# ScalarE's sigmoids of a head pair in a fixed order, and a shorter head start for the next keys, in a stick-breaking attention stage

## The chip, the cores and the metric

The kernel is one program on one core of a Trainium2 chip. Its engines are TensorE (PE in the profile; PEld is its weight load), VectorE (DVE), ScalarE (ACT), GpSimd (POOL) and SyncE (SP, whose queue issues the DMAs). The metric is the time of one execution on the device in microseconds, and smaller is better. A change is judged by the medians of the kernels before and after.

## The reference

A trunk of two layers over 512 tokens of 1024 channels: layer 0 mixes tokens by multi-scale pooling, layer 1 by stick-breaking attention with 16 heads of 64, and each is followed by a squared-ReLU MLP of 4096. All is fp32. The change lies in the attention, which is computed for blocks of 128 queries:

```python
z = jnp.einsum('bhqd,bhkd->bhqk', q_blk, k_blk, preferred_element_type=jnp.float32) * inv_sqrt_d
mask = s_idx < t_idx
log1m = jnp.where(mask, -jax.nn.softplus(z), 0.0)
excl = lax.cumsum(log1m, axis=3, reverse=True) - log1m
a = jnp.where(mask, jnp.exp(jax.nn.log_sigmoid(z) + excl), 0.0)
outs.append(jnp.einsum('bhqk,bhkd->bhqd', a, v_blk.astype(jnp.float32)))
```

So each weight is sigmoid(z) times the product of 1 - sigmoid(z) = sigmoid(-z) over the later keys.

## The kernel before

Every fp32 product is made of three matmuls on a high and a low part: high by high, high by low, low by high. Each evacuation of such an operand is therefore two instructions: ScalarE copies the high part out of PSUM, and VectorE subtracts it from the source to get the low part.

**The attention stage** runs over eight pairs of heads. TensorE works strictly in the order of `ATT_ORDER`, where each word is one step and its number the pair:

- `K` (`start`, L942) begins the projection of the keys of a pair: three of the eight blocks of 128 channels, with three matmuls each. It takes a PSUM bank that stays in use until the projection is finished.
- `P` (`queries_keys`, L962, through `project`, L947) finishes the keys and makes the queries. The copies to `kh`, `kl`, `qh`, `ql` are L967 and L968.
- `S` (`weights`, L1087) makes the scores. `scores` (L1084) fills three banks for each head: query block 3, query block 2, and blocks 1 and 0 together. The two heads alternate on TensorE. Each head then has `against` (L1007), the negated sigmoids into `u`, four instructions; `for_` (L1019), the plain sigmoids into `w`, three instructions; `scan` (L1023) on VectorE, which needs all of the head's `u`; and `weigh` (L1029) on VectorE, which multiplies `w` by the scan's result `e`. There is one buffer `e`, so the second head's scan comes after the first head's weighing.
- `T` (`transposed`) turns the weights of both heads, ten transposes for each head (L1042) into three banks, and evacuates them to `ah` and `al` (L1048 and L1052).
- `A` (`mix_pair`) multiplies by the values (L1059), one bank for each head, and copies the result out (L1066, L1070).
- `V`, `O` and `H` make values (L311 to L313, L898 and L899), output projections (L456 is their first evacuation) and the first values.

The order begins `P0 K1 S0 P1 T0 K2 S1 A0 P2 T1 K3 S2 A1 P3 O001 T2`; from pair 3 on there is no `K`, and the values' projections stand between the steps.

On the engines other than TensorE the order within this stage is chosen when the program is built, by a planner that simulates the run and takes what is ready, by the kernel's own sequence where several are. `tc.manual_schedule(engines=...)` fixes the order of the named engines to that of the code. A helper that splits weights while they are loaded has the lines L170 (ScalarE) and L172 (VectorE); a helper `split` has L292 and L293.

**PSUM** has one pool for all matmul results, with eight buffers of one bank each:

```python
psum = pool("psum", 8, space=bass.MemoryType.PSUM)
def ps():
    return psum.tile([P, 512], F32, tag="ps", name=name("ps"))
```

A buffer is handed to the next that asks once all its readers are done. The readers of a score bank are the head's `against` and `for_` of that bank.

Of the kernel before, what the change touches and what calls it, by code (L numbers as in the profile page):

```python
# [17 lines left out]
S = 512  # L18
T = S // P
KC = D // P  # L20
# [37 lines left out]

ATT_ORDER = [
    (w[0], int(w[1]), [int(c) for c in w[2:]])  # L60
    for w in """H001 N2 H101 N3 H023 H123 P0 K1 S0 P1 T0 K2 S1 A0 P2 T1 K3 S2 A1 P3 O001 T2 O023 S3 A2 P4 V20 T3 V21
    S4 A3 P5 V22 T4 V23 S5 A4 P6 V30 T5 V31 S6 A5 V323 P7 T6 E1""".split()
]

# [41 lines left out]
def trunk(ctx, tc, x, consts, grow, pw, wup, wdn, wq, wk, wv, wo, out):  # L106
# [12 lines left out]
    def name(s):  # L119
        uid[0] += 1  # L120
        return f"{s}{uid[0]}"

    def ps():
        return psum.tile([P, 512], F32, tag="ps", name=name("ps"))
# [22 lines left out]
    def gain_row(r, t=None):  # L147
        t = work.tile([P, D], F32, tag="grow", name=name("grow")) if t is None else t
        nc.sync.dma_start(t, grow[r : r + 1, :].broadcast_to((P, D)))
        return t  # L150
# [87 lines left out]
    def make():  # L238
        k, src, scaled = queue.pop(0)
        if k in kept:  # L240
            made[k] = place(k)
            for n, t in enumerate(made[k]):
                latest["sp"] = nc.sync.dma_start(t.bitcast(F32), kept[k][n])
            return
        made[k] = weight(src, place(k), scaled, dn_raw.pop(k, None))

    def fill(n=1):
        if gate[0]:
            behind.update(latest)
        for _ in range(n):  # L250
            if queue and len(made) < ahead and (queue[0][0][0] != "dn" or dn_pool[0]):
                make()

    def get(key):
        while key not in made:
            make()
        return made.pop(key)

    for l in range(2):
        if l == 1:  # L260
            n = len(queue)
# [180 lines left out]
    def need(*tiles):  # L442
        for t in tiles:
            if t in pending:
                pending.pop(t).transpose()
# [268 lines left out]
    def up_block(pu, w, cols, last=False, ks=range(KC)):  # L714
        wh = w[0].rearrange("p (k c) -> p k c", k=KC)
        wl = w[1].rearrange("p (k c) -> p k c", k=KC)

        def low(k):
            nc.tensor.matmul(pu[:, cols], wl[:, k, :], xnh[:, k, cols], start=False, stop=k == KC - 1)  # L719

        for k in ks:
            nc.tensor.matmul(pu[:, cols], wh[:, k, :], xnh[:, k, cols], start=k == 0, stop=False)  # L722
            nc.tensor.matmul(pu[:, cols], wh[:, k, :], xnl[:, k, cols], start=False, stop=False)  # L723
            if not last:
                low(k)
        if last:
            for k in range(KC):
                low(k)
# [161 lines left out]
    with tc.tile_pool(name="att", bufs=1, reuse_waits="tile") as ap:  # L890
# [14 lines left out]
        def half_values(i, part):  # L905


            if not half_w:
                half_w.extend(get(("v", 0, h)) for h in range(4))
                for u in range(2):  # L910
                    vs[u] = None, value_tile(u)
            for s in part:
                if i == 0:
                    half_bank[s] = ps()
                for k in range(4 * i, 4 * i + 4):
                    (wh, wl), c = half_w[k // 2], NS[k % 2]
                    mm3(
                        half_bank[s], xnh[:, k, TS[s]], xnl[:, k, TS[s]], wh[:, c], wl[:, c], k == 0, k == KC - 1
                    )
                if i == 1:  # L920
                    for u in range(2):
                        value_parts(vs[u][1], s, half_bank[s][:, u * 256 : u * 256 + 256])
            if i == 1 and T - 1 in part:
                fill(ahead)

        def values(u, part):
            if u not in vs:
                vs[u] = [get(("v", u, h)) for h in range(2)], value_tile(u)
            w, v = vs[u]
            for s in part:  # L930
                pv = ps()
                for k in range(KC):
                    c = slice((k % 4) * 256, (k % 4) * 256 + 256)
                    mm3(
                        pv[:, :256], xnh[:, k, TS[s]], xnl[:, k, TS[s]],
                        w[k // 4][0][:, c], w[k // 4][1][:, c], k == 0, k == KC - 1,
                    )
                value_parts(v, s, pv[:, :256])

        started = {}  # L940

        def start(key):  # L942

            started[key] = ps(), get(key)
            up_block(*started[key], slice(0, S), ks=range(3))

        def project(key):  # L947
            if key in started:
                pq, w = started.pop(key)
                up_block(pq, w, slice(0, S), ks=range(3, KC))  # L950
            else:
                pq = ps()
                up_block(pq, get(key), slice(0, S))
            return pq
# [7 lines left out]
        def queries_keys(p):  # L962
            both = []
            for what in "kq":
                src = project((what, p))
                hi, lo = qk_tile(f"{what}h"), qk_tile(f"{what}l")
                latest["act"] = nc.scalar.copy(hi, src)  # L967
                latest["dve"] = nc.vector.tensor_tensor(out=lo, in0=src, in1=hi.bitcast(F32), op=ALU.subtract)  # L968
                both.append((hi, lo))
                fill()  # L970
            return both
# [100 lines left out]
        def scores(hs, b):  # L1072


            (kh, kl), (qh, ql) = hs[0].qk
            for x in hs:
                x.pz[b] = ps()
            o = 0
            for i in Head.SCORES[b][0]:
                n = SEG[i][1]  # L1080
                for m, (x, y) in enumerate(((qh, kh), (qh, kl), (ql, kh))):
                    for h in hs:
                        own = half[h.a]
                        nc.tensor.matmul(  # L1084
                            h.pz[b][:, o : o + n], x[own, TS[i]], y[own, :n], start=m == 0, stop=m == 2,
                        )
                o += n  # L1087

        def weights(p):
            hs = [Head(qk[p], p, a) for a in range(2)]  # L1090
            for b in range(3):
                scores(hs, b)
            for x in hs:
                for b in range(3):
                    x.against(b)
            hs[0].scan()
            for x in hs:
                for b in range(3):
                    x.for_(b)
            hs[0].weigh()  # L1100
            hs[1].scan()
            hs[1].weigh()
            return hs

        def transposed(hs):
            for x in hs:
                for b in range(3):
                    x.turn(b)
                    x.high(b)
                    x.low(b)  # L1110
# [11 lines left out]
        def mix_pair(p, v):  # L1122
            o = o_tile()
            for x in heads[p]:
                x.products(v)
                x.out_low(o)
                x.out(o)
            os[p] = pair_tile(p)
            split(o, *os[p])
# [3 lines left out]
        def out_proj(u, tiles):  # L1133
            if u not in wos:
                wos[u] = [get(("o", 2 * u + c)) for c in range(2)]
            contract([os[2 * u + c] for c in range(2)], wos[u], y, u == 0, tiles)
# [115 lines left out]
        def until(key):  # L1252
            while key not in made:
                make()

        qk, heads, gpost1 = {}, {}, None

        def step(what, i, part):
            nonlocal gpost1
            if what == "H":  # L1260
                half_values(i, part)
            elif what == "V":
                values(i, part)
            elif what == "N":
                need(i)
            elif what == "K":
                start(("k", i))
            elif what == "P":
                qk[i] = queries_keys(i)
                if i == PAIRS - 1:  # L1270
                    until(("o", 5))
            elif what == "S":
                gate[0] = True
                heads[i] = weights(i)
                fill()
            elif what == "T":
                transposed(heads[i])
                behind.update(latest)
            elif what == "A":
                mix_pair(i, vs[i // 2][1])  # L1280
            elif what == "O" and part:
                out_proj(i, part)
                if gpost1 is None:
                    with tc.issue_after(latest["sp"].ins):
                        gpost1 = gain_row(R_MIX_POST1)
# [66 lines left out]
```

## Time and profile before

| | us |
|---|---|
| median of 3 runs | 953.41 (951.75 to 953.63) |
| the profiled execution, its own time | 952.13 |
| its span, first to last instruction | 950.4 |
| PE busy | 936.5 |
| DVE busy | 695.2 |
| ACT busy | 559.2 |

The span is what the trace covers; 1.7 us of the profiled execution lie around it. PE busy counts modelled ends of pipelined matmuls, so the distance between the starts of two instructions tells more than the busy time. A row of the timeline has the start, the time to the end of the last instruction of the row, the engine, the line, what is written and read, the shape and the number of instructions; in brackets stands idle time of the engine just before it and what ended that. One row can hold several instructions of a kind. Numbers of pairs are not in the rows: they follow from the order.

### The profile page before, as it was taken

How to read it: one execution, taken by the hardware profiler on the slowest of the kernel's cores; microseconds unless marked ns; L12 is line 12 of the kernel's file. 1: busy time of each engine (PE TensorE's matmuls, PEld its weight loads, DVE VectorE, ACT ScalarE, POOL GpSimd, SP SyncE). 2: the span in 40 equal slices, each digit the busy share in tenths (PEclk: the TensorE clock that was granted, in tenths of full speed). 3: DMA queues.
4: the chain of work that ended last, by engine and by line, in shares of the span. 5: the costliest groups of instructions: out<-in, count | busy, mean ns of one | idle time of the engine just before them, and what ended most of it. 6: DMA issues, size and time to landing. Idle time of an engine off the chain costs nothing.

```text
span 950.4 us, 12326 instructions
## 1 busy us (share of the span) xinstructions
PE 936.5 (99%) x4702; PEld 789.3 (83%) x4702; DVE 695.2 (73%) x797; ACT 559.2 (59%) x983; POOL 41.3 (4%) x83
## 2 busy tenths in 40 slices
PE   9999999999999999999999999999999999999996
PEld 6998888888888888877888988898888888888885
DVE  5865799988978976258466678884696966958756
ACT  6667979788775646156544444875545444444532
POOL 2300000000000004000000000200000000000002
PEclk9999999999999999999999999999999999999999
DMA  8254969789697850630434271342513233133102
GB/s 308 94 180 144 345 220 345 294 286 352 214 326 264 302 184 2 222 133 1 148 141 161 106 266 45 133 156 71 195 43 130 94 133 111 45 133 111 37 9 90
DMA packets 43262, 156.15 MB, mean 164 GB/s; under 512 B 4289, under 2 KB 4673, under 8 KB 43202
## 3 DMA queue, kind: packets, MB, share of 16 engines
q1 hardware_dynamic: 43202, 155.36, 45.9%
q8 instruction: 37, 0.61, 0.2%
q14 instruction: 23, 0.19, 0.1%
HBM read 121.79 MB, written 33.55 MB: 163 GB/s over the span
## 4 chain that ended last, share of the span: by engine, by line
PE 94%; DVE 2%; ACT 1%; DMA 1%; POOL 1%; issue 0%; SPq 0%; POOLq 0%; DVEq 0%; ACTq 0%
PE ps L600 28%; PE ps L722 15%; PE ps L719 15%; PE ps L723 15%; PE ps L311 4%; PE ps L313 4%; PE ps L312 4%; PE ps L1059 2%; PE ps L1042 2%; PE ps L1084 2%; PE ps L840 1%; PE ps L406 1%; DMA band<-in_consts 1%; PE ps L812 1%; DVE e L1023 1%; ACT xn L296 1%
## 5 line engine op out<-in xcount | busy, mean ns | idle before, releaser
L600 PE MATMUL ps<-w,a 128*128 128x512 f32 x1176 | 278.6, 389 | 0.0
L722 PE MATMUL ps<-xnh,w 128*128 128x512 f32 (+1 forms) x704 | 260.1, 371 | 0.0
L723 PE MATMUL ps<-xnl,w 128*128 128x512 f32 (+1 forms) x704 | 259.8, 370 | 0.0
L719 PE MATMUL ps<-xnh,w 128*128 128x512 f32 (+1 forms) x704 | 259.1, 370 | 0.1
L600 PEld LDWEIGHTS ps<-w,a 128*128 128x128 f32 x1176 | 220.7, 188 | 45.9
L719 PEld LDWEIGHTS ps<-xnh,w 128*128 128x128 f32 x704 | 132.2, 188 | 23.0 <-DVE w L861 0.3
L723 PEld LDWEIGHTS ps<-xnl,w 128*128 128x128 f32 x704 | 132.7, 189 | 22.1
L722 PEld LDWEIGHTS ps<-xnh,w 128*128 128x128 f32 x704 | 132.3, 188 | 22.3
L609 DVE TENSOR_TENSOR y<-ps,y 128x512 f32<-128x512 f32 x124 | 84.2, 686 | 44.1 <-PE ps L600 44.0
L172 DVE TENSOR_TENSOR w<-raw,w 128x1024 fp32r<-128x1024 f32 x58 | 70.8, 1221 | 57.0 <-ACT w L170 56.8
L170 ACT CAST w<-raw 128x1024 fp32r<-128x1024 f32 x58 | 60.9, 1050 | 81.9 <-PE ps L719 81.9
L292 ACT CAST a<-r 128x768 fp32r<-128x768 f32 (+1 forms) x60 | 47.6, 794 | 71.7 <-PE ps L600 55.2
L1023 DVE TENSOR_TENSOR_SCAN e<-u,begin 128x1280 f32<-128x1280 f32 x16 | 45.2, 2824 | 35.7 <-ACT u L1007 35.5
L293 DVE TENSOR_TENSOR a<-r,a 128x768 fp32r<-128x768 f32 (+1 forms) x60 | 54.0, 900 | 11.9 <-ACT a L292 11.8
L292 ACT CAST w<-e 128x1536 fp32r<-128x1536 f32 (+1 forms) x30 | 41.8, 1394 | 22.9 <-DVE e L574 13.5
L293 DVE TENSOR_TENSOR w<-e,w 128x1536 fp32r<-128x1536 f32 (+1 forms) x30 | 49.4, 1646 | 1.8 <-ACT w L292 1.6
L182 ACT ACTIVATE apart<-apart,eye 128x128 f32<-128x128 f32 (+1 forms) x132 | 43.1, 407 | 0.1
L293 DVE TENSOR_TENSOR w<-w,w 128x1536 fp32r<-128x1536 f32 (+1 forms) x20 | 33.0, 1649 | 8.0 <-ACT w L292 8.0
L632 ACT ACTIVATE r<-ps 128x512 f32<-128x512 f32 x56 | 33.1, 591 | 9.1 <-PE ps L719 9.1
L293 DVE TENSOR_TENSOR w<-xn,w 128x1536 fp32r<-128x1536 f32 (+1 forms) x20 | 33.0, 1650 | 5.6 <-ACT w L292 5.5
L633 ACT ACTIVATE r<-r 128x512 f32<-128x512 f32 x56 | 35.5, 634 | 1.3
L296 ACT ACTIVATE xn<-y 128x512 f32<-128x512 f32 (+1 forms) x25 | 15.3, 613 | 32.1 <-DVE y L478 28.5
(134 smaller groups left out, 1333.0 us busy)
## 6 DMA issues: line engine op xcount, KB each, us to landing
raw<-in_wup SPq DMA_DIRECT2D x64, 512.0 KB, 4.1
w<-kept SPq DMA_DIRECT2D x60, 512.0 KB, 4.2
kept<-wx SPq DMA_DIRECT2D x30, 512.0 KB, 4.4
w<-in_wdn SPq DMA_DIRECT2D x8, 1536.0 KB, 6.7
kept<-apart SPq DMA_DIRECT2D x24, 512.0 KB, 5.3
xn<-in_wdn SPq DMA_DIRECT2D x8, 1536.0 KB, 7.6
apart<-in_wk SPq DMA_DIRECT2D x7, 512.0 KB, 6.6
apart<-in_wq SPq DMA_DIRECT2D x7, 512.0 KB, 9.4
```

The costliest lines, as they stand in the source:

```text
L170: nc.scalar.copy(hi, raw)
L172: nc.vector.tensor_tensor(out=lo, in0=raw, in1=hi.bitcast(F32), op=ALU.subtract)
L182: nc.scalar.mul(c, c, gc[:, at : at + 1])
L292: latest["act"] = nc.scalar.copy(hi, src)
L293: latest["dve"] = nc.vector.tensor_tensor(out=lo, in0=src, in1=hi.bitcast(F32), op=ALU.subtract)
L311: nc.tensor.matmul(dst, ah, bh, start=start, stop=False)
L600: nc.tensor.matmul(bank, a[:, x, q, TS[t]], w[:, z, q], start=start and q == 0 and k == 0, stop=q == self.n - 1 and k == 2, skip_group_che ...
L609: nc.vector.tensor_tensor(out=part, in0=bank, in1=part, op=ALU.add)
L719: nc.tensor.matmul(pu[:, cols], wl[:, k, :], xnh[:, k, cols], start=False, stop=k == KC - 1)
L722: nc.tensor.matmul(pu[:, cols], wh[:, k, :], xnh[:, k, cols], start=k == 0, stop=False)
L723: nc.tensor.matmul(pu[:, cols], wh[:, k, :], xnl[:, k, cols], start=False, stop=False)
L1023: nc.vector.tensor_tensor_scan(out=self.e[:, ::-1], data0=self.u[:, 1:][:, ::-1], data1=begin[:, ::-1], initial=0.0, op0=ALU.mult, op1=ALU ...
```

## The change

There are two edits. The step `K` takes the number of blocks from the order, and it is two instead of three for each of the three pairs; `P` makes the other six. And in `weights` the fourteen sigmoids of a pair are in the code's order on ScalarE: all negated ones of the first head, all of the second, then the plain ones of the first head and of the second. The step `T` could now name one head alone; the order doesn't use this.

```diff
-    for w in """H001 N2 H101 N3 H023 H123 P0 K1 S0 P1 T0 K2 S1 A0 P2 T1 K3 S2 A1 P3 O001 T2 O023 S3 A2 P4 V20 T3 V21
+    for w in """H001 N2 H101 N3 H023 H123 P0 K12 S0 P1 T0 K22 S1 A0 P2 T1 K32 S2 A1 P3 O001 T2 O023 S3 A2 P4 V20 T3 V21
...
-        def start(key):
-
-            started[key] = ps(), get(key)
-            up_block(*started[key], slice(0, S), ks=range(3))
+        def start(key, n):
+
+            started[key] = ps(), get(key), n
+            up_block(*started[key][:2], slice(0, S), ks=range(n))
...
-            for x in hs:
-                for b in range(3):
-                    x.against(b)
-            hs[0].scan()
-            for x in hs:
-                for b in range(3):
-                    x.for_(b)
+            with tc.manual_schedule(engines={mybir.EngineType.Activation}):
+                for x in hs:
+                    for b in range(3):
+                        x.against(b)
+                hs[0].scan()
+                for x in hs:
+                    for b in range(3):
+                        x.for_(b)
             hs[0].weigh()
             hs[1].scan()
             hs[1].weigh()
...
-                transposed(heads[i])
+                transposed([heads[i][a] for a in part or range(2)])
```

More of the change, by code (lines that the diff above doesn't have):

```diff
@@ L940, in trunk @@
         started = {}
-        def start(key):
-            started[key] = ps(), get(key)
-            up_block(*started[key], slice(0, S), ks=range(3))
+        def start(key, n):
+            started[key] = ps(), get(key), n
+            up_block(*started[key][:2], slice(0, S), ks=range(n))
         def project(key):
             if key in started:
-                pq, w = started.pop(key)
-                up_block(pq, w, slice(0, S), ks=range(3, KC))
+                pq, w, n = started.pop(key)
+                up_block(pq, w, slice(0, S), ks=range(n, KC))
             else:
@@ L1266, in step @@
             elif what == "K":
-                start(("k", i))
+                start(("k", i), *part)
             elif what == "P":
```

## The prediction

> **What bounds the kernel.** I read the page first, then TensorE's waits within the attention stage, then the timelines of TensorE, ScalarE and VectorE around those waits. The page, and the waits of TensorE from 395 to 600 us:
>
> ```profile
> span 950.4 us, 12326 instructions
> PE 936.5 (99%) x4702; PEld 789.3 (83%) x4702; DVE 695.2 (73%) x797; ACT 559.2 (59%) x983; POOL 41.3 (4%) x83
> ...
> PE ps L1042 <- DVE w L1029: 4.3, 2, 2.3
> ```
>
> TensorE is the bound, and an edit on ScalarE pays only where TensorE waits. Two waits stand out, both of a turn (L1042) for VectorE's weighing (L1029). The weight loads show their size, and a third, smaller one:
>
> ```profile
> 419.41 1.08 PEld L1042 LDWEIGHTS ps<-eye,w 128*128 128x128 f32 x10 [2.49 <-issue]
> 439.61 1.07 PEld L1042 LDWEIGHTS ps<-eye,w 128*128 128x128 f32 x10 [2.28 <-ACT ah L1048]
> 444.61 0.18 PEld L1084 LDWEIGHTS ps<-kh,qh 64*128 64x128 f32 x1 [0.34 <-DVE al L1052]
> ```
>
> These are the second heads of T0 and T1, 2.49 and 2.28 us, together 4.77, and the third score bank of S2. TensorE's starts agree, and give the lengths that I need:
>
> ```profile
> 414.99 0.39 PE L719 MATMUL ps<-xnh,w 128*128 128x512 f32 x1
> ...
> 415.67 0.39 PE L719 MATMUL ps<-xnh,w 128*128 128x512 f32 x1
> 415.90 1.25 PE L1042 MATMUL ps<-eye,w 128*128 128x128 f32 x10
> 419.44 1.28 PE L1042 MATMUL ps<-eye,w 128*128 128x128 f32 x10 [2.28 <-DVE w L1029]
> ...
> 488.96 2.35 PE L1042 MATMUL ps<-eye,w 128*128 128x128 f32 x20
> 491.06 0.36 PE L311 MATMUL ps<-w,xnh 128*128 128x256 f32 x1
> ```
>
> Three projection matmuls, one eighth, take 0.68 us (414.99 to 415.67). Twenty unhindered turns take 2.10, so ten take 1.05: the second head's turns were wanted at 416.95 and began at 419.44.
>
> **What T0 waits for.** VectorE and ScalarE on the first pair:
>
> ```profile
> 405.87 0.60 ACT L1007 ACTIVATE u<-ps 128x511 f32<-128x511 f32 x1 [2.35 <-PE ps L1084]
> ...
> 409.28 1.08 ACT L1007 ACTIVATE u<-ps 128x255 f32<-128x255 f32 x4
> 410.01 2.83 DVE L1023 TENSOR_TENSOR_SCAN e<-u,begin 128x1280 f32<-128x1280 f32 x1 [5.76 <-ACT u L1007]
> 412.94 1.49 DVE L1029 TENSOR_TENSOR w<-w,e 128x1280 f32<-128x1280 f32 x1
> ...
> 414.95 2.82 DVE L1023 TENSOR_TENSOR_SCAN e<-u,begin 128x1280 f32<-128x1280 f32 x1
> 417.80 1.49 DVE L1029 TENSOR_TENSOR w<-w,e 128x1280 f32<-128x1280 f32 x1
> ```
>
> A serial chain: first scan, weighing, second scan, weighing, turn. It starts at 410.01, 4.14 us after the first sigmoid, since the planner took negated and plain sigmoids in turn and the first head's small ones came only at 409.28. The scan starts 0.73 after them.
>
> **The new ScalarE order, by the rows of the next pair.**
>
> ```profile
> 423.72 0.60 ACT L1007 ACTIVATE u<-ps 128x511 f32<-128x511 f32 x1 [2.27 <-PE ps L1084]
> 424.22 0.59 ACT L1019 ACTIVATE w<-ps 128x512 f32<-128x512 f32 x1
> 424.69 0.60 ACT L1007 ACTIVATE u<-ps 128x511 f32<-128x511 f32 x1
> 425.17 0.62 ACT L1019 ACTIVATE w<-ps 128x512 f32<-128x512 f32 x1
> 425.65 0.52 ACT L1007 ACTIVATE u<-ps 128x383 f32<-128x383 f32 x1
> 426.02 0.53 ACT L1019 ACTIVATE w<-ps 128x384 f32<-128x384 f32 x1
> ...
> 427.13 1.08 ACT L1007 ACTIVATE u<-ps 128x255 f32<-128x255 f32 x4
> 427.97 1.00 ACT L1019 ACTIVATE w<-ps 128x384 f32<-128x384 f32 x2
> ```
>
> By start to start a large sigmoid takes 0.50 or 0.48, a middle one 0.37, a head's two small ones 0.42 (0.84 for four). TensorE's side of that pair:
>
> ```profile
> 422.72 0.50 PE L1084 MATMUL ps<-kh,qh 64*128 64x512 f32 x2
> ...
> 424.58 0.27 PE L1084 MATMUL ps<-kh,ql 64*128 64x128 f32 x2
> 424.78 0.50 PE L1059 MATMUL ps<-ah,v 128*128 128x512 f32 x1
> ...
> 426.11 0.44 PE L1059 MATMUL ps<-ah,v 128*128 128x512 f32 x1
> ```
>
> Count from the first sigmoid. The third bank is done at 424.58 + 0.27 - 423.72 = 1.13, so the first head's small sigmoids start at 1.16 (0.03 for the hand-over) and end at 1.58, with about 0.27 idle before them. The scan starts at 1.16 + 0.73 = 1.89 instead of 4.14: 2.25 earlier. The second head's negated ones fill 1.58 to 2.85 (0.48 + 0.37 + 0.42), and only then comes the first plain one, 2.85 to 3.44 (0.59).
>
> **Term 1, T0: -2.49.** With one eighth fewer ahead of it, S0 starts 0.68 earlier; T0's first head stays at 415.90, since the eighth moves behind S0. The last weighing so ends 2.25 + 0.68 = 2.93 earlier and allows the second head's turns at 416.51, before the wanted 416.95. The whole wait goes, with 0.44 to spare; if VectorE's low part of the keys is placed worse, up to 0.7 of it stays.
>
> **Term 2, T1: -2.28.** Here too the scan comes 2.25 earlier after the scores, the eighth gives 0.68, and term 3 delays the turns and not the chain. I take the whole wait. Between the weighings stand two additions of L1070 and a weight split (L172), whose places the planner may change; if that splits the chain, about 1 us stays.
>
> **Term 3, a new wait: +2.3.** In S1 and S2 all eight PSUM banks are taken when the second head's products (L1059) want theirs: one by the begun keys, six by scores, one by the first head's products. The first to come free is the first head's large score bank, and its last reader is now the plain sigmoid that ends at 3.44 (before, at 424.22 + 0.59 - 423.72 = 1.09). The products want it at 426.11 - 423.72 = 2.39. With 0.1 for the hand-over that is 1.15 us in A0 and again in A1. Behind it on TensorE stand those products and all of the next P. Bounds: 1.05 without hand-over, 1.4 with the 0.15 from weighing (417.80 + 1.49) to turn (419.44) and 0.2 of delay in the sigmoids.
>
> The Trainium skill, "ScalarE: Activation LUTs", What ACT_TABLE_LOAD costs, gives an ACTIVATE 186 ns + 0.833 ns per column and an overlap of about 93 ns; by it the plain sigmoid would end near 3.7 and this term would be 2.8. The rows are shorter (0.48 us where it gives 0.52 for 511 columns), and the sum goes by them.
>
> From pair 3 on nothing holds a bank for begun keys, and the products find one. But the first matmul behind the products takes that score bank, that of the next keys or, after A5, of the values:
>
> ```profile
> 471.50 0.60 ACT L1007 ACTIVATE u<-ps 128x511 f32<-128x511 f32 x1 [0.36 <-PE ps L1084]
> ...
> 475.11 0.45 PE L722 MATMUL ps<-xnh,w 128*128 128x512 f32 x1
> ```
>
> It wants it 3.61 after the first sigmoid; the bank comes at 3.54. I take 0; from 0 to 0.15 for each of four pairs.
>
> **Term 4, S2: +0.45.** Fewer eighths lie between a turn and the next scores, which need the banks that VectorE's low parts (L1052) empty.
>
> ```profile
> 436.32 1.25 PE L1042 MATMUL ps<-eye,w 128*128 128x128 f32 x10
> 437.06 1.05 ACT L170 CAST w<-raw 128x1024 fp32r<-128x1024 f32 x1
> 440.62 1.22 DVE L172 TENSOR_TENSOR w<-raw,w 128x1024 fp32r<-128x1024 f32 x1
> 441.75 3.14 DVE L1052 TENSOR_TENSOR al<-ps,ah 128x512 fp32r<-128x512 f32 x6
> 442.93 0.50 PE L1084 MATMUL ps<-kh,qh 64*128 64x512 f32 x2
> 444.26 0.73 PE L1084 MATMUL ps<-kh,qh 64*128 64x256 f32 x2
> ```
>
> Around T1 a weight split stands ahead of the low parts. From the start of T1's turns its ScalarE part ends at 437.06 + 1.05 - 436.32 = 1.79, VectorE's takes 1.13 (440.62 to 441.75), and the fifth low part releases the third score bank 2.86 after the first (441.75 to 444.61): 5.78. Unhindered turns (2.10), six key matmuls with their gaps (2.23 for nine after T0, less 0.68: 1.55) and two score banks (442.93 to 444.26, 1.33) bring TensorE there at 4.98: a wait of 0.8, with restart 0.9. Before it was about 0.46 (S2's scores took 2.52 to the products, S1's 2.06). So +0.45; with the split placed later -0.46, and +0.7 at worst. After T0 there is no split, and the same reckoning leaves 0.6 to spare. S0's own scores need the low part of the queries, ready about 0.4 before its use even with one eighth less. Matmul, sigmoid and DMA counts stay, and no DMA is moved past another.
>
> **Sum.** -2.49 - 2.28 + 2.3 + 0.45 = -2.0 on 952.13, the profiled execution: 950.1. The median lies 1.28 above that execution: 951.4. By the bounds it goes from -3.1 (waits of 1.05, S2 free of its wait) to +1.0 if all bad ones fell together (0.7, 1.0, 0.5, 0.6 and 0.25 more); I take half of these, so its own range is -3.1 to -0.5, 950.3 to 952.9. A change of 0.2% is 1.9 us, about what a measurement of this kernel can tell from no change, so the forecast itself lies at that edge.
>
> **Rivals.** *A bank is free after all* in A0 and A1, and only terms 1, 2 and 4 count: -4.3, 949.1. For it: the wait isn't in the trace of before, where the bank came free at 1.09. Against it: the count of eight.
>
> *Every pair pays for the late banks: slower.* The place is the products of A0 and A1 and the first matmul behind A2 to A5. If the bank handed out is one released by the second head's plain sigmoid, it comes at 3.44 + 0.48 + 0.37 + 0.37 = 4.66 and a hand-over: 2.35 in A0 and A1, and 4.75 - 3.61 = 1.15 at four pairs, together 9.3; with -4.77 + 0.45 that is +5.0, 958.4. It decides from the point where the banks' waits pass 4.3 us in sum. Against it: the first head's bank does come free first. The Trainium skill speaks for it: "PSUM — Partial Sum Buffer", Summary, asks to empty banks promptly, and the change reads every first-head bank twice, far apart; that pairs 3 to 6 have slack of 0.07 only, by the rows above, agrees.
>
> *The chain does not move.* If the planner sets VectorE's work so that the early scan is followed by other work, only the eighth counts: 0.68 of each turn's wait goes, S2 costs 0.45: -0.9, 952.5.
>
> **Chances.** Forecast 0.56, no bank wait 0.12, every pair pays 0.17, chain unmoved 0.10, 0.05 for a replan elsewhere. Of the forecast a little over half lies beyond 1.9 us: 0.32, with the first rival and a share of the rest 0.46 faster; 0.24 + 0.10 is 0.34 within; 0.20 slower. The range of 948.9 to 954.2 takes in the forecast with its bounds and both rivals that end below, and leaves out the slower one.
>
> **What would show it.** Right: no wait for L1029 in T0 and T1, the first scan about 1.9 us after the first sigmoid, a wait of 1.1 us within L1059 twice, a longer S2. Wrong: a wait for L1029 that stays, products without a wait, or waits of the first matmuls behind A2 to A5 for ScalarE.

## The result, and the profile after

| | before | after |
|---|---|---|
| median, us | 952.39 (951.75 to 953.72, 11 runs) | 950.39 (950.27 to 950.99, 11 runs) |
| span of the profiled execution, us | 950.4 | 948.6 |

The ratio is 0.9976, with a 95% interval of 0.9967 to 0.9985: the change makes the kernel 2.0 us faster by the medians and 1.8 by the spans; forecast was 2.0. The eleven times of before fall in two groups, 951.75 to 952.39 and 953.38 to 953.72, so its median can move by 1 us from one set of runs to the next, while those of the changed kernel lie within 0.7 us. The page of the changed kernel, and TensorE's waits from 395 to 600 us:

```profile
span 948.6 us, 12348 instructions
...
PE ps L1059 <- ACT w L1019: 2.1, 2, 1.1
PE ps L1084 <- DVE al L1052: 0.2, 1, 0.2
PE ps L406 <- ACT xn L396: 0.2, 1, 0.2
```

The last row, a norm's 0.2 us, was there before as well. The turns (L1042) no longer wait for the weighing. Instead the products with the values (L1059) wait for ScalarE's plain sigmoids (L1019), twice. TensorE's timeline in the first two pairs:

```profile
415.83 2.35 PE L1042 MATMUL ps<-eye,w 128*128 128x128 f32 x20
...
419.50 0.49 PE L1084 MATMUL ps<-kh,qh 64*128 64x512 f32 x2
...
421.56 0.50 PE L1059 MATMUL ps<-ah,v 128*128 128x512 f32 x1
...
424.13 0.50 PE L1059 MATMUL ps<-ah,v 128*128 128x512 f32 x1 [1.08 <-ACT w L1019]
425.45 0.45 PE L722 MATMUL ps<-xnh,w 128*128 128x512 f32 x1
...
435.08 2.35 PE L1042 MATMUL ps<-eye,w 128*128 128x128 f32 x20
...
438.75 0.53 PE L1084 MATMUL ps<-kh,qh 64*128 64x512 f32 x2
...
441.74 0.50 PE L1059 MATMUL ps<-ah,v 128*128 128x512 f32 x1
```

T0 and T1 are rows of 20 turns without a break, where before each was cut in two. The weight loads show the size of what is left:

```profile
424.13 0.19 PEld L1059 LDWEIGHTS ps<-ah,v 128*128 128x128 f32 x1 [1.22 <-ACT w L1019]
438.75 0.21 PEld L1084 LDWEIGHTS ps<-kh,qh 64*128 64x128 f32 x2 [0.36 <-DVE al L1052]
440.90 0.18 PEld L1084 LDWEIGHTS ps<-kh,qh 64*128 64x128 f32 x1 [0.41 <-DVE al L1052]
444.21 0.19 PEld L1059 LDWEIGHTS ps<-ah,v 128*128 128x128 f32 x1 [1.11 <-ACT w L1019]
```

ScalarE and VectorE, where the order can be read:

```profile
405.10 3.03 ACT L1007 ACTIVATE u<-ps 128x511 f32<-128x511 f32 x8 [1.67 <-PE ps L1084]
407.96 2.68 ACT L1019 ACTIVATE w<-ps 128x512 f32<-128x512 f32 x6
...
421.72 1.87 ACT L1007 ACTIVATE u<-ps 128x255 f32<-128x255 f32 x6 [0.16 <-PE ps L1084]
423.42 2.68 ACT L1019 ACTIVATE w<-ps 128x512 f32<-128x512 f32 x6
```

```profile
406.91 2.83 DVE L1023 TENSOR_TENSOR_SCAN e<-u,begin 128x1280 f32<-128x1280 f32 x1 [2.75 <-ACT u L1007]
...
411.37 2.83 DVE L1023 TENSOR_TENSOR_SCAN e<-u,begin 128x1280 f32<-128x1280 f32 x1
414.11 0.67 DVE L968 TENSOR_TENSOR kl<-ps,kh 128x512 fp32r<-128x512 f32 x1
414.69 1.48 DVE L1029 TENSOR_TENSOR w<-w,e 128x1280 f32<-128x1280 f32 x1
...
430.90 1.49 DVE L1029 TENSOR_TENSOR w<-w,e 128x1280 f32<-128x1280 f32 x1
...
432.91 1.22 DVE L172 TENSOR_TENSOR w<-raw,w 128x1024 fp32r<-128x1024 f32 x1
```

Eight negated sigmoids run ahead of six plain ones, and the first scan starts 1.81 us after the first sigmoid (406.91 - 405.10), where it was 4.14.

A ledger of starts, after less before, shows where the time went. Beside the rows above and those of the forecast it needs one more of the kernel before, the first matmul behind A0:

```profile
427.38 0.45 PE L722 MATMUL ps<-xnh,w 128*128 128x512 f32 x1
```

T0 starts 0.07 earlier (415.83, 415.90). S1 starts 3.22 earlier (419.50, 422.72): 2.47 of T0's wait, and 0.68 of keys moved behind the scores. The first matmul behind A0 is 1.93 earlier (425.45, 427.38): 1.29 were given back. T1 is 1.24 earlier (435.08, 436.32; the moved eighth is back), S2 4.18 (438.75, 442.93): T1 brought 2.26. Then S2's longer wait and A1's wait take their part, and the span ends 1.8 earlier.

### The profile page after: what moved, and what is told of

Read it like the earlier page. It is cut to its first block, busy times and chain, and to the rows that moved or that the text cites. A ratio compares the mean times of both kernels' runs of the same rounds, so it can differ in the third digit from the quotient of the medians.

```text
span 948.6 us, 12348 instructions
## 1 busy us (share of the span) xinstructions
PE 937.6 (99%) x4702; PEld 789.9 (83%) x4702; DVE 696.4 (73%) x797; ACT 560.4 (59%) x983; POOL 41.1 (4%) x83
## 4 chain that ended last, share of the span: by engine, by line
PE 96%; ACT 1%; DVE 1%; POOL 1%; issue 0%; POOLq 0%; DVEq 0%; ACTq 0%
PE ps L600 28%; PE ps L722 15%; PE ps L719 15%; PE ps L723 15%; PE ps L311 4%; PE ps L312 4%; PE ps L313 4%; PE ps L1059 2%; PE ps L1042 2%; PE ps L1084 2%; PE ps L840 1%; PE ps L406 1%; PE ps L812 1%; PE ps L767 1%; ACT xn L296 1%; ACT u L1007 0%
```

## The experiments

The theory is that of the forecast. The early scan removes TensorE's waits in T0 and T1, and the price is one PSUM bank: in A0 and A1 all eight are taken, and the second head's products get the first head's large score bank only after its last reader, the plain sigmoid, which the new order puts behind the second head's negated ones. The rivals: the shorter head start carries the gain; or the products wait for ScalarE's load, or something else, and not for that bank.

| kernel | median, us | ratio to before, 95% |
|---|---|---|
| the change | 950.39 | 0.9976 (0.9967 to 0.9985) |
| order only | 949.93 | 0.9960 (0.9948 to 0.9973) |
| head start only | 951.50 | 0.9983 (0.9974 to 0.9992) |
| bank freed early | 947.72 | 0.9940 (0.9927 to 0.9952) |
| bank freed early, 3/8 for pair 3 | 947.06 | 0.9932 (0.9919 to 0.9944) |
| bank freed early, 3/8 for all | 947.43 | 0.9935 (0.9922 to 0.9947) |
| no head start for pairs 2 and 3 | 949.38 | 0.9961 (0.9947 to 0.9974) |
| one sigmoid more | 952.94 | 0.9998 (0.9989 to 1.0007) |
| one sigmoid more, bank freed early | 947.49 | 0.9937 (0.9925 to 0.9950) |

The kernel before was run beside each group; its medians were 952.39 beside the change, 953.05 beside the next four rows as far as three eighths for pair 3, and 953.55 beside the last four. The ratios are the record's own estimate and not the quotients of these medians; the two differ by up to 0.07%, so ratios of different groups are compared here only to about 0.1%. In the traces T0 itself starts anywhere from 415.48 to 416.38 us. No edit touches a wait ahead of T0, so what an edit does is read from waits within the stage, and not from spans alone.

**Order only.** The fixed order, with three eighths (in `K13` the first digit is the pair, the second the number of eighths).

```diff
-P0 K12 S0 P1 T0 K22 S1 A0 P2 T1 K32 S2
+P0 K13 S0 P1 T0 K23 S1 A0 P2 T1 K33 S2
```

> Only the fixed ScalarE order; the next keys keep three eighths ahead of the scores. Against the kernel before, by theory: the scans still come 2.25 us earlier, so T1's wait (2.28) goes and T0's falls from 2.49 to 0.0-0.2 (in the changed kernel the second weighing left 0.55 to spare, and one eighth is 0.68); the two bank waits in A0 and A1 stay, 1.15 to 1.25 each; S2 waits 0.2 instead of 0.46. Sum -2.4 to -2.6: 949.9, about 0.5 faster than the whole change. Rival (the shorter head start is what makes the early scan pay): T0 keeps 0.7 or more, and the kernel is 0.5 or more slower than the whole change, 951 or above.

It came to 949.93. In its timeline of the weight loads the two bank waits stand as in the change, and the late row of S2 is gone:

```profile
425.25 0.19 PEld L1059 LDWEIGHTS ps<-ah,v 128*128 128x128 f32 x1 [1.23 <-ACT w L1019]
439.89 0.18 PEld L1084 LDWEIGHTS ps<-kh,qh 64*128 64x128 f32 x2 [0.36 <-DVE al L1052]
...
442.18 0.19 PEld L1059 LDWEIGHTS ps<-ah,v 128*128 128x128 f32 x1
...
444.66 0.19 PEld L1059 LDWEIGHTS ps<-ah,v 128*128 128x128 f32 x1 [1.14 <-ACT w L1019]
```

T0's twenty turns and the next key matmul lie 2.23 apart (416.14 to 418.37) instead of 2.10: T0 waits 0.13. S2's scores take 2.29 us to the products (439.89 to 442.18), in the change 2.99 (438.75 to 441.74). So the order alone brings the whole gain. Against the whole change the intervals of the ratios overlap; it is the trace that shows what the shorter head start costs, 0.70 in S2 less 0.13 in T0.

**Head start only.** The planner orders ScalarE, with two eighths.

```diff
-            with tc.manual_schedule(engines={mybir.EngineType.Activation}):
-                for x in hs:
+            for x in hs:
...
```

> Only the shorter head start, two eighths; ScalarE's order is left to the planner as before. By theory it merely moves 0.68 us from one side of the scores to the other: T0's wait 1.81 and T1's 1.60, no bank waits in A0 and A1, and S2's wait grows from 0.46 to about 1.1, since VectorE's low parts come no earlier. Sum -0.7 against before: 951.7. Rival (the head start carries the gain): 950.4, as the whole change.

951.50, near the expected 951.7. But the kernel before had 953.05 beside it, so by the medians the gain was 1.5 and not 0.7 us (1.1 by the spans, 950.4 to 949.3), and the waits are not all where they were expected:

```profile
418.32 1.08 PEld L1042 LDWEIGHTS ps<-eye,w 128*128 128x128 f32 x10 [1.81 <-ACT ah L1048]
436.75 1.07 PEld L1042 LDWEIGHTS ps<-eye,w 128*128 128x128 f32 x10 [0.46 <-issue]
438.43 0.19 PEld L722 LDWEIGHTS ps<-xnh,w 128*128 128x128 f32 x1 [0.60 <-DVE kl L968]
...
440.76 0.18 PEld L1084 LDWEIGHTS ps<-kh,qh 64*128 64x128 f32 x1 [0.56 <-DVE al L1052]
442.88 0.18 PEld L1084 LDWEIGHTS ps<-kh,qh 64*128 64x128 f32 x1 [0.41 <-DVE al L1052]
```

T0's wait is the expected 1.81. T1's is 0.46 and not 1.60, because the planner now put the weight split and the low part of the keys behind the second weighing of that pair (436.55 and 437.69, behind 435.15), and these came late in turn: the next keys wait 0.60 for a bank, and S2 waits twice. Its scores take 3.69 us to the products (440.02 to 443.71), before 2.52. That the waits still sum to the forecast is luck: -0.68 in T0, -1.82 in T1, +0.60 and +1.17 make -0.73, and the rest of the shorter span, 0.40, lies ahead of T0 (415.50, before 415.90). The gains of the two edits do not add: both shorten the same waits.

**Bank freed early.** One plain sigmoid is moved ahead of the second head's negated ones.

```diff
-                for x in hs:
-                    for b in range(3):
-                        x.against(b)
+                for b in range(3):
+                    hs[0].against(b)
+                hs[0].for_(0)
+                for b in range(3):
+                    hs[1].against(b)
                 hs[0].scan()
```

> The whole change with one plain sigmoid moved: that of the first head's large bank comes right behind the first head's negated ones, ahead of the second head's. By theory the large bank then comes free 2.3 us after the first sigmoid, just before the second head's products want it (2.40), so both bank waits (1.25 and 1.15) go down to 0.0-0.1, the scan stays where it is, and nothing takes their place: -2.3 against the change, 948.1. Rival (the products wait for ScalarE's pace or for another buffer, not for that bank): waits within L1059 stay near 1.1 each and the time is that of the change, 950.4.

947.72. The products of A0 follow each other at the unhindered distance, 1.32 us, where the change had 2.57 (421.56 to 424.13). ScalarE's and then TensorE's rows:

```profile
421.54 0.55 ACT L1007 ACTIVATE u<-ps 128x255 f32<-128x255 f32 x2 [0.16 <-PE ps L1084]
421.97 0.61 ACT L1019 ACTIVATE w<-ps 128x512 f32<-128x512 f32 x1
422.45 1.44 ACT L1007 ACTIVATE u<-ps 128x511 f32<-128x511 f32 x4
```

```profile
421.39 0.50 PE L1059 MATMUL ps<-ah,v 128*128 128x512 f32 x1
...
422.71 0.45 PE L1059 MATMUL ps<-ah,v 128*128 128x512 f32 x1
```

The plain sigmoid ends at 422.58, 0.13 before the products start, so the bank comes just in time. The other five plain sigmoids come as late as in the change and cost nothing. Nothing took the place of the two waits.

**Bank freed early, three eighths for pair 3.** In addition `K32` becomes `K33`.

> As the last, and three eighths again for pair 3 alone, the pair whose scores waited 0.5 us for VectorE's low parts behind a weight split. By theory S2's wait falls by 0.5 and T1 has 2 us to spare for the 0.68: 947.6, the fastest of the four. Rival (S2's wait is for something that moves along, or T1's turns wait again): 948.1 or slower.

947.06, the lowest median of all. TensorE's waits from 395 to 600 us are down to the norm's:

```profile
PE ps L406 <- ACT xn L396: 0.2, 1, 0.2
```

Against the last the gain of 0.66 us is not resolved by the intervals, but the traces show it: the row that S2's wait had left in the change (440.90) has no counterpart, and S2's scores take 2.29 to the products (438.43 to 440.72), in the last 2.99 (437.27 to 440.26).

**Bank freed early, three eighths for all.** `K13`, `K23` and `K33`.

> The order with the large bank freed early, and three eighths for all three pairs, as before the change. By theory the order with three eighths had no wait in T0, so nothing is lost: 947.1, as with three eighths for pair 3 alone. Rival (two eighths are needed for pair 1): a wait of up to 0.7 in T0, 947.7.

947.43, not to be told from the last, and halfway between what was expected and the rival. T0 loses about 0.13 as in the order alone (415.71 to 417.94, 2.23), where the expectation had put nothing; S2 still shows a short wait here:

```profile
439.93 0.18 PEld L1084 LDWEIGHTS ps<-kh,qh 64*128 64x128 f32 x1 [0.41 <-DVE al L1052]
```

**No head start for pairs 2 and 3.** No begun keys hold a bank.

```diff
-T0 K22 S1 A0 P2 T1 K32 S2
+T0 S1 A0 P2 T1 S2
```

> The whole change, but the keys of pairs 2 and 3 get no head start at all (their projection is made whole in the next step P). So no begun keys hold a bank while the products of A0 and A1 want theirs. By theory both bank waits go to 0 without any edit of ScalarE's order; in exchange the scores follow right on the turns and wait for VectorE's low parts: about 0.8 in S1 (fifth low part 2.9 us after the first, against 2.1 + 1.3 from the turns) and 2.0 to 2.3 in S2. In sum 0 to +0.8 against the change: 950.4 to 951.2. Rival (the products wait for ScalarE itself, whatever banks are free): the two waits of 1.1 stay and the scores' waits come on top, 953 or more.

The two bank waits are gone, with ScalarE's order as in the change: it is the count of eight banks that makes them. The size was a miss, 949.38 instead of 950.4 to 951.2. The weight loads with a wait, and the first matmul of A1's products:

```profile
418.65 0.19 PEld L1084 LDWEIGHTS ps<-kh,qh 64*128 64x128 f32 x2 [0.17 <-ACT ah L1048]
436.75 0.19 PEld L1084 LDWEIGHTS ps<-kh,qh 64*128 64x128 f32 x2 [0.17 <-ACT ah L1048]
438.17 0.18 PEld L1084 LDWEIGHTS ps<-kh,qh 64*128 64x128 f32 x1 [0.90 <-DVE al L1052]
438.77 0.18 PEld L1084 LDWEIGHTS ps<-kh,qh 64*128 64x128 f32 x1 [0.41 <-DVE al L1052]
439.70 0.18 PEld L1084 LDWEIGHTS ps<-kh,qh 64*128 64x128 f32 x1 [0.41 <-DVE al L1052]
...
440.54 0.50 PE L1059 MATMUL ps<-ah,v 128*128 128x512 f32 x1
```

S1 hardly waits (2.25 us to the products, before 2.06), and S2's scores take 3.79 us to the products (436.75 to 440.54), 0.80 more than in the change. The bank that the begun keys no longer hold also serves the scores, so their last wait is for the fourth low part where I had counted the fifth. That explanation is read from the times and the count of banks, and no further run was made for it. With 2.4 us of bank waits less, 0.8 more in S2 and 0.2 in S1, the stage should be 1.4 us ahead of the change. The medians and the spans differ by 1.0; T0 starts 0.55 later in this trace (416.38, in the change 415.83).

**One sigmoid more.** The second head's large negated sigmoid is made twice, ahead of all plain ones.

```diff
+                hs[1].against(0)
                 hs[0].scan()
```

> The whole change with one large sigmoid more for every pair (the second head's negated one of the large bank is made a second time, ahead of the plain ones): 0.48 us of ScalarE before the first bank comes free. By theory A0 and A1 wait 0.48 longer each, 1.7 and 1.6, and behind A2 to A5, where the next matmul takes that bank with 0.1 to 0.15 to spare, a new wait of 0.3 to 0.4 appears four times: +2.2 to +2.6 against the change, 952.8, so that the change would be worth nothing. Rival (only A0 and A1 feel the bank): +1.0, 951.4. Second rival (ScalarE has slack and no bank matters): 950.4.

952.94: 0.48 us of work for each pair costs 2.55 us in all by the medians (2.3 by the spans), and the gain is gone. The bank waits of A0 and A1 grow to 1.64 and 1.56, and behind A2, A3, A4 and A5 the expected four new ones appear, to be read in TensorE's timelines there:

```profile
474.49 0.50 PE L722 MATMUL ps<-xnh,w 128*128 128x512 f32 x1 [0.25 <-ACT w L1019]
...
498.56 0.50 PE L722 MATMUL ps<-xnh,w 128*128 128x512 f32 x1 [0.23 <-ACT w L1019]
...
522.64 0.50 PE L722 MATMUL ps<-xnh,w 128*128 128x512 f32 x1 [0.24 <-ACT w L1019]
...
546.72 0.39 PE L311 MATMUL ps<-w,xnh 128*128 128x256 f32 x1 [0.23 <-ACT w L1019]
```

By starts they are 0.42, 0.39, 0.40 and 0.39 (behind A2, 473.96, the last matmul of the products, to 474.49 is 0.53, where the change has 0.11), together 1.60. With 0.42 and 0.45 more in A0 and A1 that is 2.5.

**One sigmoid more, bank freed early.** The same extra sigmoid, behind the early plain one.

> The order with the large bank freed early, and the same extra large sigmoid for every pair, behind the early plain one. By theory the extra work is free here, since the bank is free before it and the second scan starts 3 us later: 947.7 to 947.9, no waits within L1059, none behind A2 to A5. Rival (ScalarE's load is what the stage pays for): +1 to +2.6 against that order, 948.7 or more.

947.49, against 947.72 without it: free. Its trace has no wait within L1059 and none behind A2 to A5. So ScalarE's load isn't what the stage pays for; the time at which one bank comes free is.

## Why the prediction was right

**The sum.** The terms came out at -2.47, -2.26, +2.38 by starts (1.24 in A0, 1.14 in A1) and +0.47, together -1.9 for the forecast -2.0; the profiled executions differ by 1.74 (952.13, 950.39). That the medians differ by just 2.0 is in part luck. The forecast median was 951.4, since the median of the three runs lay 1.28 above the profiled execution; that of eleven lies 0.26 above, and the changed kernel's 950.39 came near the lower end of the forecast's own range, 950.3 to 952.9.

**T0 and T1.** Both waits went whole, 2.47 and 2.26 us by the ledger for 2.49 and 2.28. The scan came 1.81 after the first sigmoid (1.89 in the working). VectorE put the low part of the keys between the second scan and its weighing (414.11), not ahead of the scan; the spare time at T0 was about 0.55 and not 0.44. T1 had far more: the weight split went behind the second weighing (432.91), not between the two, and that weighing ended at 432.39, while the second head's turns were wanted at 436.13.

**The new wait.** It is where it was put, 1.22 and 1.11 at the weight loads for 1.15 each. The plain sigmoid began at 423.42; with its 0.59 and a hand-over of 0.12 the products started at 424.13. The durations by the rows carried it. As an estimate by the figures of the Trainium skill, "ScalarE: Activation LUTs", What ACT_TABLE_LOAD costs, each wait would have been 1.4.

**S2.** Its scores took 2.99 to the products (438.75 to 441.74), before 2.52: +0.47 for +0.45. The weight split does stand ahead of the low parts, as reckoned.

**Pairs 3 to 6.** No wait behind A2 to A5, for the 0 that was taken; the extra sigmoid, 0.48 long, made waits of 0.39 to 0.42 there, so the slack is under 0.1.

**The rivals.** A free bank after all: no, two waits of 1.1. Every pair pays: not in the change, but half a microsecond of extra sigmoid brings it about in small, with waits of 0.4 at four pairs where that rival had 1.15. The Trainium skill, "PSUM — Partial Sum Buffer", Summary, has the rule to empty banks promptly; the 2.55 us there, and the two waits, 2.33 us, that went with the early bank, agree with it for the one bank that is wanted next. For the other five score banks, emptied late at no cost in the early-bank order, no run here shows it. An unmoved chain: no. The forecast lay at the edge of 0.2%, and so does the measurement. One thing the working didn't say: the shorter head start was taken as part of the gain, while it only costs some 0.6 us once the scan is early. The working had the numbers for it: without the eighth's 0.68, T0 would have lacked 0.24 (0.44 to spare less 0.68), and S2 would not have paid 0.45. The traces give 0.13 and 0.70.

## What to carry to other kernels

When an order is changed so that one consumer gets its input sooner, list what the delayed instructions were releasing: here six of eight PSUM banks hung on the plain sigmoids, and half of the 4.7 us was paid back for one of them. Between two goals in one queue, place the single instruction that frees the scarce buffer first, and leave the others behind: that gave 0.6% where the change gave 0.24%. Two edits that shorten the same wait should be measured apart, since after the first the second may only cost.

## What was unexpected

Nothing in the hardware. That an edit of the order on TensorE alone (head start only) moved VectorE's weight split to the other side of a weighing, and left T1 a wait of 0.46 us where 1.6 was expected, comes from the planner. A forecast by rows of such a kernel needs a margin of about 1 us for it. Whether more is to be had by ordering VectorE in the same way was not tried.
